# The high and low parts of turned tiles take a place in the weights' line beside w_down's first tiles

## The chip, the cores and the metric

The kernel runs on one core of a Trainium2 chip. A core has five engines with instruction queues of their own: TensorE (PE; its weight loads are shown as PEld), VectorE (DVE), ScalarE (ACT), GpSimd (POOL) and SyncE (SP). PE multiplies into PSUM; DVE and ACT do elementwise work; SP, ACT and POOL issue DMA transfers, and here nearly all loads of weights are issued by SP. The metric is the device time of the whole program in microseconds, the median of several runs.

## What is computed

One decoder layer on 256 tokens of width 2048, in float32. The parts that matter here are the last two lines, cut from the reference:

```python
h = h + rmsnorm(mix, norm_mix_post)                       # mixer: SSD heads beside attention heads
ff = squared_relu_mlp(rmsnorm(h, norm_mlp_pre), w_up, w_down)
h = h + rmsnorm(ff, norm_mlp_post)

def squared_relu_mlp(u, w_up, w_down):
    hdn = relu(u @ w_up)          # 2048 -> 8192
    return (hdn * hdn) @ w_down   # 8192 -> 2048
```

## The kernel before

**Products of parts.** Every float32 product is made of three products of shortened parts. A matrix is split into a high part, rounded by ACT (line 150), and a low part, the rest, which DVE subtracts (line 151): `split`. PE then adds high x high, high x low and low x high. Weights arrive in pairs of 128-row blocks (a k-pair) by 512 columns, 512 KB, in a buffer named `raw` or in one lent from elsewhere (`ha`, `uc`, `mw`). Their parts go into `hi` and `lo`, of which there are five pairs.

**Two kinds of tiles.** A k-pair is multiplied either directly (`row_tiles`: 24 matmuls for two column blocks and two blocks of tokens) or by Strassen's seven products (`seven`: 21 matmuls). A Strassen tile loads a block `raw_a` for one set of columns and `raw_b` for the other; the first piece of raw_b comes from a buffer in DRAM (`pair`) in which POOL has added two blocks ahead of time. DVE makes sums `e` and `t4` of these blocks (line 275), and four splits follow. The sums of the activations are made by `sums_of_acts` (lines 428 to 431).

**Units.** `unit` works through one pair of column blocks: an order of k-pairs, some direct and some by Strassen, then a few last ones directly; before these, the Strassen sums are combined (`combine_new`, `combine_onto`). The layer's MLP runs in two halves of 4096 hidden columns. In each half units for w_up follow one another, then two units for w_down; the second one of the second half ends the kernel. The first w_down unit of each half has 14 k-pairs in its order and the k-pairs 14 and 15 as last ones.

**Turned tiles.** The hidden activations leave w_up with tokens along the partitions; w_down needs them with features there. A unit for w_up leaves four tiles, two blocks of tokens by two of columns. Each is worked on in two steps (`turned`, a generator): `pump_beside` starts it (ReLU and square on ACT, a copy on ACT that puts the 16-bit halves of its words into a buffer named `halves`, and a DMA transposition issued by SP), and `land_beside` finishes it (a copy back into `halves`, then a `split` of the whole tile, 128x512, into the activations' high and low parts, named `sh`/`sl` or `ah`/`al`). This is done beside the tiles of the next unit, at places given by `TURNS` and `LANDS`. The four tiles of the last w_up unit of a half are started and finished beside the first w_down unit, the landings standing behind its tiles 5, 7, 9 and 11. These units have orders longer than seven, and for them `room["exact"]` is true; the landing behind tile 0 has it false, and so have those beside w_up.

**The order of the instructions.** The program is written in one order, and a planner sorts each engine's queue by priority and by when it expects operands. `tc.high_priority(offset=AHEAD)` lifts what stands in it; all work on weights stands in such a block. Beside that there is a line: `split_in_line` and `add_in_line` put an instruction behind the last ACT and the last DVE instruction of the line (`tc.issue_after`), and become the last ones themselves. All weights that `fetch_next` brings are split in the line. With `room["exact"]`, the two copies of a turned tile are in the line as well (line 1515 in `perhaps_in_line`), with high priority; without it, they are not (line 1512). The split of the turned tile is not in the line, nor has it high priority: it only stands behind the newest ACT instruction of the line when it is written.

**Buffers.** `fetch_next` walks a ring of four `raw` buffers and the lent ones in `room["raw"]`. In the second half's first w_down unit `room["chain"]` is set: each transfer is issued behind the one before. When the last of the four turned tiles has landed, `more_in_place` adds the two buffers that held `halves` to this ring (`spare_a`, `of_halves`). The k-pair behind the fourth landing is k = 12, the one after it the Strassen tile k = 13.

Of the kernel before, what the change touches and what calls it, by code (L numbers as in the profile page):

```python
# [10 lines left out]
F32 = mybir.dt.float32  # L11
# [33 lines left out]
AHEAD = 1_000_000  # L45
# [35 lines left out]
def hymba_layer(ctx: ExitStack, tc: tile.TileContext, x, norm_mix_pre, w_in, conv_w, conv_b, dt_bias, a_log,  # L81
# [34 lines left out]
    def part(k):  # L116
        if k < NK:
            return sh, sl, k
        i, r = divmod(k - NK, NK // 2)
        return (*att[i], r)  # L120
# [26 lines left out]
    def split(hi, lo, src, scale=None):  # L147

        if scale is None:
            return (nc.scalar.activation(hi, src, AF.Copy),  # L150
                    nc.vector.tensor_tensor(lo, src, hi.bitcast(F32), op=ALU.subtract))  # L151
        return (nc.scalar.activation(hi, src, AF.Copy, scale=scale),
                nc.vector.scalar_tensor_tensor(lo, src, scale, hi.bitcast(F32), op0=ALU.mult, op1=ALU.subtract))
# [27 lines left out]
    room = {}  # L181
# [78 lines left out]
    @contextmanager  # L260
    def in_line():

        with ExitStack() as order:
            for last in line.values():
                order.enter_context(tc.issue_after(last.ins))
            yield

    def split_in_line(hi, lo, raw):
        with in_line():
            line["act"], line["dve"] = split(hi, lo, raw)  # L270
            newest["act"] = line["act"]
# [683 lines left out]
    def attention(ap, h, qT, kT, v):  # L955
# [30 lines left out]
        for j, p in enumerate(turned):  # L986
            pair[j] = ap.tile([P, 3 * P], F32, name="pT", bufs=4)
            nc.scalar.activation(pair[j], p[:, :3 * P], AF.Copy)
# [181 lines left out]
    def mix_to_up(c0, ks, acc):  # L1170
# [38 lines left out]
        def turn(t, n):  # L1209
            if len(banks) < 3:  # L1210
                banks.append([bank() if banks else psmall() for _ in range(2)])
            p = turned[t, n] = banks[len(turned) % 3]
            for f in range(4):
                k = 4 * n + f
                nc.tensor.transpose(p[f % 2][:, f // 2 * P:(f // 2 + 1) * P], of_h(t, slice(k * P, (k + 1) * P)), ident)
# [284 lines left out]
    def up_end(fb, b):  # L1500

        def at_end(t, acc):
            with tc.high_priority(offset=AHEAD):
                r = room["shared"][b][t]
                nc.vector.tensor_tensor(r, acc, r, op=ALU.subtract if b else ALU.add)
            beside.append(turned(t, 4 * fb, r))
        return at_end

    def perhaps_in_line(dst, src):

        if not room["exact"]:
            nc.scalar.activation(dst, src, AF.Copy)
            return
        with tc.high_priority(offset=AHEAD), in_line():
            newest["act"] = line["act"] = nc.scalar.activation(dst, src, AF.Copy)

    def turned(t, k, r):
        room["halves"].rotate(1)
        halves = room["halves"][0]
        ts = slice(t * P, (t + 1) * P)  # L1520
        words = r.bitcast(U16)
        nc.scalar.activation(r, r, AF.Relu, scale=rmlp[:, t:t + 1])
        nc.scalar.activation(r, r, AF.Square)
        perhaps_in_line(halves.rearrange("p (h n) -> p h n", h=2), words.rearrange("p (n h) -> p h n", h=2))
        nc.sync.dma_start_transpose(words.rearrange("p (n s) -> p n s", s=P), halves)
        yield
        perhaps_in_line(halves.rearrange("p (n h) -> p h n", h=2), words.rearrange("p (h n) -> p h n", h=2))
        d_h, d_l, i = part(k)
        split(d_h[:, i:i + 4, ts], d_l[:, i:i + 4, ts], halves.bitcast(F32).rearrange("p (f s) -> p f s", f=4))

    def onto_new_mw(more):

# [98 lines left out]
```

## Time and profile before

| | us |
|---|---|
| median of 3 runs | 1460.96 (1460.77 to 1460.99) |
| the profiled execution | 1460.29 |
| its span, first to last instruction | 1458.5 |
| PE busy in the span | 1437.7 |
| DVE busy | 1297.9 |
| ACT busy | 1001.3 |
| w_down's first unit of the first half, PE | about 937.5 to 1026.7 |
| the same of the second half | about 1272.5 to 1367.9 |

The profile is of one execution. A row of a timeline gives start and duration in microseconds, the engine, the line of the code, the operation, what is written and read, the shape and a count; the brackets at its end tell how long the engine was idle ahead of it and what ended that. A row of waits gives who waited for whom, the total, the number of times and the longest. A row "<- DMA" names a transfer; SPq is SP's queue of transfers. A line can be that of a helper: 150 and 151 are all splits, and the tiles' names tell which.

### The profile page before, as it was taken

The numbers are of one execution on the slowest core, as the hardware profiler recorded it, in microseconds if no ns is written. First come the engines' busy times: TensorE is split into PE (matmuls) and PEld (weight loads), VectorE is DVE, ScalarE is ACT, GpSimd is POOL, SyncE is SP. The second block draws the span as 40 slices with busy tenths as digits, with TensorE's granted clock in tenths as the row PEclk, the third lists the DMA queues.
The fourth block names the chain that finished last, engine by engine and source line by source line (L and its number), as shares of the span: only waits on it lengthen the run. The fifth ranks groups of instructions, "written<-read, shape, count | busy, mean of one in ns | idle before, by whom it ended". The sixth has DMA issues, their size and how long they took to land.

```text
span 1458.5 us, 20230 instructions
## 1 busy us (share of the span) xinstructions
PE 1437.7 (99%) x6930; PEld 1207.1 (83%) x6930; DVE 1297.9 (89%) x1881; ACT 1001.3 (69%) x1407; POOL 162.3 (11%) x244
## 2 busy tenths in 40 slices
PE   9999999999999999999999999999999999998998
PEld 8888888888888888888888888887888888876786
DVE  6798888988999788689989999999889999987998
ACT  6577669666666666566657679976565799876564
POOL 0201110131111000011100111010111111001000
PEclk9999999999999999999999999999999999999999
DMA  7977656756888647588976799698788999998855
GB/s 256 276 218 225 186 173 185 238 173 195 235 249 244 196 131 237 183 270 262 267 232 211 222 342 291 186 256 273 203 252 263 266 268 278 254 259 250 275 181 173
DMA packets 201926, 340.30 MB, mean 233 GB/s; under 512 B 45616, under 2 KB 48544, under 8 KB 201824
## 3 DMA queue, kind: packets, MB, share of 16 engines
q1 hardware_dynamic: 174304, 279.72, 61.4%
q0 software_dynamic: 19648, 45.63, 15.5%
q10 hardware_dynamic: 7872, 13.68, 2.8%
q8 instruction: 54, 0.88, 0.2%
q14 instruction: 48, 0.39, 0.1%
HBM read 327.39 MB, written 49.84 MB: 259 GB/s over the span
## 4 chain that ended last, share of the span: by engine, by line
PE 65%; DVE 6%; ACT 3%; issue 2%; DMA 2%; SPq 0%; DVEq 0%; ACTq 0%
PE acc L384 9%; PE acc L382 9%; PE acc L383 9%; PE acc L469 6%; PE acc L470 6%; PE acc L471 6%; PE acc L540 4%; DVE lo L151 3%; PE ps L384 2%; PE ps L382 2%; PE ps L383 2%; PE acc L543 2%; PE ps L471 2%; PE ps L470 2%; PE ps L469 2%
## 5 line engine op out<-in xcount | busy, mean ns | idle before, releaser
L151 DVE TENSOR_TENSOR lo<-raw,hi 128x1024 fp32r<-128x1024 f32 (+1 forms) x392 | 475.4, 1217 | 84.6 <-ACT hi L150 82.5
L150 ACT ACTIVATE hi<-raw 128x1024 fp32r<-128x1024 f32 (+1 forms) x392 | 408.0, 1048 | 181.6 <-PE acc L384 58.1
L540 PE MATMUL acc<-ua,hi 128*128 128x512 f32 x520 | 142.1, 402 | 0.0
L150 ACT ACTIVATE hi<-e 128x1024 fp32r<-128x1024 f32 x66 | 70.0, 1061 | 61.0 <-DVE e L275 55.5
L540 PEld LDWEIGHTS acc<-ua,hi 128*128 128x128 f32 x520 | 91.8, 190 | 14.1
L382 PE MATMUL acc<-hi,ua 128*128 128x512 f32 x228 | 90.0, 395 | 0.0
L383 PE MATMUL acc<-lo,ua 128*128 128x512 f32 x228 | 89.2, 391 | 0.0
L384 PE MATMUL acc<-hi,ua 128*128 128x512 f32 x228 | 89.1, 391 | 0.0
L382 PE MATMUL acc<-hi,sh 128*128 128x512 f32 x220 | 86.4, 393 | 0.0
L384 PE MATMUL acc<-hi,sl 128*128 128x512 f32 x220 | 85.7, 389 | 0.0
L383 PE MATMUL acc<-lo,sh 128*128 128x512 f32 x220 | 85.6, 389 | 0.0
L543 PEld LDWEIGHTS acc<-ua,lo 128*128 128x128 f32 x520 | 77.0, 190 | 9.0
L151 DVE TENSOR_TENSOR lo<-e,hi 128x1024 fp32r<-128x1024 f32 x66 | 80.4, 1217 | 0.9 <-ACT hi L150 0.7
L543 PE MATMUL acc<-ua,lo 128*128 128x256 f32 x520 | 79.2, 282 | 0.0
L469 PE MATMUL acc<-hi,ah 128*128 128x512 f32 x180 | 70.1, 390 | 4.1 <-ACT hi L150 4.1
L470 PE MATMUL acc<-lo,ah 128*128 128x512 f32 x180 | 70.4, 391 | 0.0
L471 PE MATMUL acc<-hi,al 128*128 128x512 f32 x180 | 70.3, 390 | 0.0
L540 PE MATMUL acc<-uc,hi 128*128 128x512 f32 x208 | 61.4, 405 | 0.0
L150 ACT ACTIVATE hi<-ha 128x1024 fp32r<-128x1024 f32 x46 | 48.2, 1051 | 15.8 <-DMA ha<-in_w_down_dram 6.2
L151 DVE TENSOR_TENSOR lo<-ha,hi 128x1024 fp32r<-128x1024 f32 x46 | 55.7, 1218 | 2.7 <-ACT hi L150 2.6
L150 ACT ACTIVATE hi<-r 128x512 fp32r<-128x512 f32 x66 | 41.2, 625 | 18.3 <-PE acc L384 8.5
L469 PE MATMUL acc<-hi,ua 128*128 128x512 f32 x137 | 53.5, 390 | 0.0
(578 smaller groups left out, 3739.0 us busy)
## 6 DMA issues: line engine op xcount, KB each, us to landing
raw<-in_w_in_dram SPq DMA_DIRECT2D x154, 512.0 KB, 4.6
raw<-in_w_down_dram SPq DMA_DIRECT2D x70, 512.0 KB, 5.4
raw<-in_w_up_dram SPq DMA_DIRECT2D x65, 512.0 KB, 5.1
raw<-in_w_out_dram SPq DMA_DIRECT2D x38, 512.0 KB, 5.1
raw<-pair SPq DMA_DIRECT2D x61, 256.0 KB, 4.3
pair<-in_w_up_dram POOLq DMA_DIRECT2D x56, 256.0 KB, 6.1
pair<-in_w_down_dram POOLq DMA_DIRECT2D x52, 256.0 KB, 5.8
ha<-in_w_up_dram SPq DMA_DIRECT2D x25, 512.0 KB, 5.7
```

The costliest lines, as they stand in the source:

```text
L150: return (nc.scalar.activation(hi, src, AF.Copy), nc.vector.tensor_tensor(lo, src, hi.bitcast(F32), op=ALU.subtract))
L151: nc.vector.tensor_tensor(lo, src, hi.bitcast(F32), op=ALU.subtract))
L382: nc.tensor.matmul(dst[:, cs], a_h[:, r, ts], hi[:, j, cs], start=begin and j == 0, stop=False)
L383: nc.tensor.matmul(dst[:, cs], a_h[:, r, ts], lo[:, j, cs], start=False, stop=False)
L384: product[t] = nc.tensor.matmul(dst[:, cs], a_l[:, r, ts], hi[:, j, cs], start=False, stop=end and j == KB - 1)
L469: nc.tensor.matmul(dst, a_h, hi[:, j], start=own and first, stop=False)
L470: nc.tensor.matmul(dst, a_h, lo[:, j], start=False, stop=False)
L471: nc.tensor.matmul(dst, a_l, hi[:, j], start=False, stop=own and last)
L540: nc.tensor.matmul(acc[f], hi[:, j, f * P:(f + 1) * P], u(k0 + j), start=k0 + j == 0, stop=False, skip_group_check=True)
L543: nc.tensor.matmul(acc[f][:, 0], lo[:, j, f * P:(f + 1) * P], u(k0 + j)[:, 0], start=False, stop=k0 + j == NK - 1, skip_group_check=True)
```

## The change

When `room["exact"]` is set, the split of a landed turned tile is made by `split_in_line` in a block of high priority; otherwise it is made as before.

```diff
         yield
         perhaps_in_line(halves.rearrange("p (n h) -> p h n", h=2), words.rearrange("p (h n) -> p h n", h=2))
         d_h, d_l, i = part(k)
-        split(d_h[:, i:i + 4, ts], d_l[:, i:i + 4, ts], halves.bitcast(F32).rearrange("p (f s) -> p f s", f=4))
+        whole = halves.bitcast(F32).rearrange("p (f s) -> p f s", f=4)
+        if not room["exact"]:
+            split(d_h[:, i:i + 4, ts], d_l[:, i:i + 4, ts], whole)
+            return
+        with tc.high_priority(offset=AHEAD):
+            split_in_line(d_h[:, i:i + 4, ts], d_l[:, i:i + 4, ts], whole)
```

`split_in_line` is as it was:

```python
def split_in_line(hi, lo, raw):
    with in_line():
        line["act"], line["dve"] = split(hi, lo, raw)
        newest["act"] = line["act"]
```

## The prediction

> **What bounds the kernel now.** The profiled execution took 1460.29 us; its span is 1458.5. I read the page first, then what TensorE (PE) waited for over the whole span, then the timelines around its longest waits on PE, VectorE (DVE), ScalarE (ACT) and SP's DMA queue.
>
> ```profile
> span 1458.5 us, 20230 instructions
> PE 1437.7 (99%) x6930; PEld 1207.1 (83%) x6930; DVE 1297.9 (89%) x1881; ACT 1001.3 (69%) x1407; POOL 162.3 (11%) x244
> ...
> PE acc L469 <- ACT hi L150: 5.7, 2, 4.1
> PE ps L384 <- DVE al L151: 3.4, 1, 3.4
> PE ps L383 <- DVE lo L151: 2.2, 4, 0.8
> ```
>
> PE bounds nearly everything. Two places carry most of its waits: one of 3.4 us for `al`, the low part of a turned tile, and two of 5.7 us together for high parts of weights. The first lies beside the first w_down tiles of the first half, the others beside those of the second half, just where turned tiles are split. First half, PE's timeline, then two stretches (busy times, granted clock, DMA share, GB/s):
>
> ```profile
> 1011.92 0.39 PE L382 MATMUL acc<-hi,ah 128*128 128x512 f32 x1
> 1012.15 0.39 PE L383 MATMUL acc<-lo,ah 128*128 128x512 f32 x1
> 1015.98 0.50 PE L384 MATMUL ps<-hi,al 128*128 128x512 f32 x1 [3.44 <-DVE al L151]
> 1020.66 0.39 PE L384 MATMUL ps<-hi,al 128*128 128x512 f32 x1
> ...
> 1016.00:1020.00 4.00, 4.00 (x12) 3.14 (x13) 2.54 (x5) 1.65 (x2) 0.55 (x1) 0.64 0.95 337
> 1303.00:1307.00 4.00, 2.92 (x12) 1.88 (x11) 3.17 (x7) 4.00 (x5) 0.55 (x1) 1.00 0.91 287
> ```
>
> Unhindered matmuls start about every 0.227 us (the first two rows, rounded there). From 1012.15 to 1020.66 lie 14 starts, worth 3.18 us, in 8.51: **5.3 us are lost**, 3.6 in the gap and 1.7 in a stretch at 0.64 of the clock. The second stretch holds the longest wait on a weight's low part, 0.8 us, and kept the clock at 1.00. What ACT and DVE did:
>
> ```profile
> 989.91 0.61 ACT L150 ACTIVATE ah<-mw 128x512 fp32r<-128x512 f32 x1
> 999.76 0.61 ACT L150 ACTIVATE ah<-mw 128x512 fp32r<-128x512 f32 x1
> ...
> 1010.15 2.35 DVE L151 TENSOR_TENSOR lo<-raw,hi 128x1024 fp32r<-128x1024 f32 x2
> 1014.10 1.22 DVE L151 TENSOR_TENSOR lo<-raw,hi 128x1024 fp32r<-128x1024 f32 x1 [1.60 <-ACT hi L150]
> 1015.24 1.28 DVE L151 TENSOR_TENSOR al<-mw,ah 128x512 fp32r<-128x512 f32 x2
> ```
>
> Both high parts were ready by 1000.4, yet their low parts stand behind every low part of weights, even one (1014.10) that waited for its own high part and belongs to the next unit: this unit's last four are the ones up to 1012.5. PE waited for 1.28 us of work that could have been done over 10 us earlier. Second half:
>
> ```profile
> 1343.39 0.39 PE L384 MATMUL acc<-hi,al 128*128 128x512 f32 x1
> 1347.89 0.50 PE L469 MATMUL acc<-hi,ah 128*128 128x512 f32 x1 [4.11 <-ACT hi L150]
> 1350.36 0.80 PE L469 MATMUL acc<-hi,ub 128*128 128x512 f32 x1 [1.55 <-ACT hi L150]
> 1355.16 0.39 PE L470 MATMUL acc<-lo,ub 128*128 128x512 f32 x1
> ...
> 1352.00:1355.00 3.00, 3.00 (x9) 2.32 (x8) 1.77 (x3) 2.49 (x3) 0.80 (x1) 0.50 0.94 327
> ...
> 1333.51 1.37 ACT L1515 ACTIVATE ha<-wpost 128x1024 uint16<-128x1024 uint16 x1
> 1336.62 0.61 ACT L150 ACTIVATE ah<-ha 128x512 fp32r<-128x512 f32 x1
> 1346.78 1.06 ACT L150 ACTIVATE hi<-ha 128x1024 fp32r<-128x1024 f32 x1 [6.17 <-DMA ha<-in_w_down_dram]
> ...
> 1335.04 0.68 DVE L151 TENSOR_TENSOR lo<-r,hi 128x512 fp32r<-128x512 f32 x1
> 1339.06 0.68 DVE L151 TENSOR_TENSOR al<-ha,ah 128x512 fp32r<-128x512 f32 x1
> 1339.86 0.68 DVE L151 TENSOR_TENSOR al<-ha,ah 128x512 fp32r<-128x512 f32 x1
> 1350.82 1.22 DVE L151 TENSOR_TENSOR lo<-e,hi 128x1024 fp32r<-128x1024 f32 x1
> ...
> 1338.96 0.37 SPq L164 DMA_DIRECT2D ha<-in_w_down_dram  x1
> 1340.57 0.37 SPq L164 DMA_DIRECT2D ha<-in_w_down_dram  x1
> SPq L164 <- DVE al L151: 1.2, 1, 1.2
> 1341.49 6.88 DMA raw<-in_w_down_dram
> ```
>
> Here the lateness acts through SP. After the fourth landing the buffers through which tiles were turned become weight buffers, and the next Strassen tile's raw_a (k = 13) goes into one of them. Its transfer was issued at 1340.57, right behind the last `al`; raw_b is chained behind it, and its second piece, issued at 1341.49, took 6.88 us. From 1343.39 to 1355.16 lie 14 starts, worth 3.18 us, in 11.77: **8.6 us are lost**, waits and half the clock together. SP had issued the transfer at 1338.96, one for the next unit, ahead of it.
>
> **The change part by part.** Eight pairs of splits, four in each half, get high priority and a place in the line: the high part on ACT right behind the copy back (L1515, in the line already), the low part on DVE in the weights' order. No instruction and no DMA is added or removed.
>
> The first two pairs of each half follow their copies closely already. They change places with neighbours whose sum stays the same: nothing. The third and fourth move.
>
> *The first half's wait.* Both `al` would be done near 1000. What is late next are the low parts of this unit's last weights, done at 1012.5, or 1.2 later with the push below; PE then has most of 40 matmuls (9 us) ahead of the last of them, which covers it. Gain 5.3.
>
> *The push.* Two low parts move ahead of weights on a DVE that runs there without a gap; each costs 0.60 (1.28 less the 0.68 of one). The rows of the k-pair behind the fourth landing:
>
> ```profile
> 998.45 1.22 DVE L151 TENSOR_TENSOR lo<-mw,hi 128x1024 fp32r<-128x1024 f32 x1
> 1000.36 0.39 PE L382 MATMUL ps<-hi,ah 128*128 128x512 f32 x1
> ...
> 1336.25 1.22 DVE L151 TENSOR_TENSOR lo<-ha,hi 128x1024 fp32r<-128x1024 f32 x1
> 1338.18 0.39 PE L382 MATMUL ps<-hi,ah 128*128 128x512 f32 x1
> ```
>
> With 1.2 more the low part ends at 1000.87, and PE's second matmul wants it at 1000.59: a wait of 0.3. In the second half 1338.67 against 1338.41, again 0.3. Bounds of each: 0, if low-priority sums give way, and 1.2, all of the push. ACT's high parts move too, by some 0.5 each, hidden in the 31% that ACT is idle; without that cover it is the same push once more.
>
> *The transfer.* The fourth copy ends at 1334.9. Behind it come its high part and, after the low part that now ends near 1336.3, its `al`, done near 1336.9 in place of 1340.54. raw_a goes out at 1337.0, raw_b's second piece at 1337.9, as far behind as before. The planner can issue raw_a as soon as its model sees the buffer free, and the line frees it ahead of the k = 12 weights' buffers, for which the next unit's transfers wait. How long the piece then takes:
>
> ```profile
> raw<-in_w_down_dram SPq DMA_DIRECT2D x19, 256.0 KB, 4.7
> ```
>
> Between 4.7 (median of its kind) and 6.88; I take 5.5, since fewer transfers stand ahead of it. It lands at 1343.4. Before, the low part of `e` ended 3.67 after that landing (1350.82 + 1.22 less 1348.37): 1347.1. At full speed PE wants it at 1343.39 + 0.23 + 0.3 + 7 x 0.227 = 1345.5. A wait of 1.6 stays, 0.8 to 3.0 by the bounds. Whether a wait of 1.6 costs clock no row shows; 0.8 did not and 3.4 did, for 1.7. It is nearer to 0.8, so 0, with 1.7 as the other end.
>
> The Trainium skill (TensorE: Matmul & The Clock Gate, "HAM oscillation — how this bites in real kernels") warns of PE gaps above about 3.4 us and not of shorter ones. By that the remaining wait has no such tail and the sum stands; a gate that acts at 1.6 already would make it 10.0. The trace agrees at both ends, 0.8 and 3.4.
>
> *The sum.* 5.3 + 8.6 - 0.3 - 0.3 - 1.6 = **11.7 us**. Span 1446.8, that execution 1448.6, and the median of the runs, 0.67 above it, **1449.3**. With all costs at their lower ends the gain is 13.1 (1447.9); at their upper ends, 5.3 + 8.6 - 1.2 - 1.2 - 3.0 - 1.7 = 6.8 (1454.2).
>
> That the first half's 5.3 reaches the end needs the weights to keep ahead of an earlier PE. ACT's waits from 1040 to 1060 and from 1360 to 1380:
>
> ```profile
> ACT hi L150 <- PE acc L384: 4.9, 4, 2.1
> ACT hi L150 <- PE acc L384: 4.5, 3, 1.7
> ```
>
> Behind both places ACT waits for PE to free weight buffers. Preparation is as far ahead as its buffers allow, so everything later moves with PE.
>
> **The rivals.** *SP keeps its order* (0.13): the planner leaves raw_a behind the transfer at 1338.96, whose buffer is pushed by 1.2; raw_a gains nothing, the second half loses 8.6 as before. Gain 5.3 - 0.6 = 4.7: 1456.3. For it speaks that the planner did put that transfer first; against it, that the buffer is now free earlier in any model, since the line fixes it.
>
> *The first gain is swallowed* (0.09) by the up phase of the second half, where DVE is nearly full: gain 11.7 - 5.0 = 6.7, 1454.3. Against it stand the waits for buffers.
>
> *It does not do what it says* (0.07): the low parts stay where they are, because the planner still sees their copies late. 1461. Against it: L1515 is the in-line copy, and the splits take their order from it.
>
> *Slower* (0.06): the line holds both engines at a late copy. Now DVE's weights, too, queue behind an `al` that waits for a copy that waits for its transposition. Each of eight landings would cost PE the lateness; above 1.5 us each (11.7 / 8) the kernel is slower. SP's transpositions of the second half already waited for ACT, 2.2 us each:
>
> ```profile
> SPq L1525 <- ACT hi L150: 8.9, 4, 3.8
> ```
>
> At 2.2 each, 1449.3 + 17.6 = 1466.9. Against it: the copy at 1333.51 has no idle time before it. The Trainium skill (TensorE: Matmul & The Clock Gate, opening table) calls the queues of ACT and DVE strict FIFO, which is what would make this bite; the first half's `al` behind a waiting low part agrees.
>
> **How the numbers follow.** The forecast has 0.65, with a range of its own from 1446 to 1454. The range from 1445 to 1457.5 adds the first two rivals and, below, the chance that the small waits for low parts (2.2 us) shrink too; it leaves out the last two and a little more. Faster, same and slower mean by more than 0.2%, 2.9 us, about what can be told here: 0.86, 0.08, 0.06.
>
> **What would show it.** Right: no PE wait for `al`; each `al` within 2 us behind its high part; raw_a's issue before 1338 and before the next unit's second transfer; no stretch under full clock near 1016 or 1350; small new waits for low parts behind the landings. Wrong: a DMA wait over 3 us at k = 13 (SP's order), new waits of PE in the up phase of the second half (swallowed), or idle ACT time before L1515 (the slower rival).

## The result, and the profile after

The changed kernel takes **1449.95 us** (median of 4 runs, 1449.0 to 1453.54) against 1460.97 (4 runs, 1460.77 to 1462.45): a ratio of 0.9927, 95% interval 0.9908 to 0.9946. That is 11.0 us faster. The profiled execution took 1449.0. Timed again on another chip, the same kernel had 1450.74 (6 runs) against 1459.61 (18 runs), 0.9946 (0.9931 to 0.9962), so 8.9 us. The gain is sure; its size is known to some 3 us either way.

The page of the changed kernel, span and busy times:

```profile
span 1446.7 us, 20233 instructions
...
PE 1432.2 (99%) x6930; PEld 1202.3 (83%) x6930; DVE 1298.3 (90%) x1881; ACT 1002.8 (69%) x1407; POOL 162.4 (11%) x244
```

What PE waited for (in total, times, longest):

```profile
PE acc L469 <- ACT hi L150: 2.3, 2, 1.5
PE ps L382 <- ACT hi L150: 1.9, 3, 0.7
PE ps L383 <- DVE lo L151: 1.8, 3, 0.8
```

The same work is done. DVE, ACT and POOL are busy as long as before, to within 1.5 us. PE is busy for 5.5 us less (1437.7 before): from the first w_down unit on, the old profile had two stretches at half clock, 3.41 and 6.83 us long, and this one has none. The row for `al` is gone, the waits of L469 have shrunk from 5.7 to 2.3, and those of L382 have grown (0.7 before).

**Where the 11.8 us between the two spans lie.** The first matmul of three units is easy to find in both timelines: w_down's first unit of the first half, the unit that follows it, and w_down's first unit of the second half. Before:

```profile
937.50 0.39 PE L382 MATMUL ps<-hi,sh 128*128 128x512 f32 x1
...
1026.80 0.39 PE L382 MATMUL acc<-hi,sh 128*128 128x512 f32 x1
...
1272.47 0.39 PE L382 MATMUL ps<-hi,sh 128*128 128x512 f32 x1
```

After:

```profile
936.05 0.39 PE L382 MATMUL ps<-hi,sh 128*128 128x512 f32 x1
...
1020.91 0.39 PE L382 MATMUL acc<-hi,sh 128*128 128x512 f32 x1
...
1266.62 0.39 PE L382 MATMUL ps<-hi,sh 128*128 128x512 f32 x1
```

The differences of these starts, and what is left up to the span's end:

| us | before | after | gain |
|---|---|---|---|
| start to the first place | 937.50 | 936.05 | 1.45 |
| first place (w_down's first unit) | 89.30 | 84.86 | 4.44 |
| between (second unit, up phase) | 245.67 | 245.71 | -0.04 |
| second place to the end | 186.03 | 180.08 | 5.95 |

The first 1.45 us lie ahead of all changed instructions: the old kernel's profiled execution had a slower start. The other profiles start this place between 935.03 and 936.09, whether their kernel has the change or not. So the 1.45 us aren't the change's, and the two places gave 10.4 us between these two executions.

**The first place.** The changed kernel's timeline on ACT, DVE and PE at the fourth landing, and two stretches of PE's time where the old kernel waited until 1015.98 and then ran at 0.64 of the clock (busy times, granted clock, DMA share, GB/s):

```profile
997.06 0.63 ACT L150 ACTIVATE ah<-mw 128x512 fp32r<-128x512 f32 x1
998.41 0.68 DVE L151 TENSOR_TENSOR al<-mw,ah 128x512 fp32r<-128x512 f32 x1
999.35 1.22 DVE L151 TENSOR_TENSOR lo<-mw,hi 128x1024 fp32r<-128x1024 f32 x1
999.62 0.62 PE L382 MATMUL ps<-hi,ah 128*128 128x512 f32 x2
1000.07 0.61 PE L382 MATMUL acc<-hi,ah 128*128 128x512 f32 x2
1000.60 0.50 PE L469 MATMUL acc<-hi,ah 128*128 128x512 f32 x1
1000.93 0.39 PE L383 MATMUL ps<-lo,ah 128*128 128x512 f32 x1
```

```profile
1008.00:1012.00 4.00, 4.00 (x19) 3.34 (x18) 4.00 (x7) 2.92 (x3) 0.00 (x0) 1.00 0.99 252
1012.00:1016.00 4.00, 4.00 (x20) 3.30 (x19) 4.00 (x5) 1.67 (x2) 0.00 (x0) 1.00 0.52 165
```

`al` is done at 999.1, not at 1016.5, and PE is busy without a gap at full clock. The weights' low part now ends at 1000.57, and no wait stands before the matmul that wants it at 1000.93: five products of high parts come first, where the old order had one.

**The second place.** The chain of waits of the changed kernel (start, duration, what):

```profile
1330.45 0.70 DVE al L151
...
1331.16 0.37 SPq L164
...
1331.59 0.46 SPq L159
...
1332.09 6.80 DMA raw<-in_w_down_dram
...
1338.99 0.70 DVE e L275
...
1339.78 1.07 ACT hi L150
...
1340.89 0.50 PE acc L469
```

The same stretch on PE's timeline, and the granted clock behind it:

```profile
1337.48 0.39 PE L384 MATMUL acc<-hi,al 128*128 128x512 f32 x1
1338.63 0.50 PE L469 MATMUL acc<-hi,ah 128*128 128x512 f32 x1 [0.77 <-ACT hi L150]
...
1340.89 0.50 PE L469 MATMUL acc<-hi,ub 128*128 128x512 f32 x1 [1.52 <-ACT hi L150]
...
1343.50 0.39 PE L470 MATMUL acc<-lo,ub 128*128 128x512 f32 x1
```

```profile
1339.00:1342.00 3.00, 1.48 (x7) 0.94 (x6) 3.00 (x4) 2.22 (x3) 0.00 (x0) 1.00 1.05 405
1342.00:1345.00 3.00, 3.00 (x15) 2.46 (x14) 3.00 (x5) 3.00 (x5) 0.29 (x1) 1.00 1.05 412
```

raw_a goes out right behind `al`, but the chain is the old one: `al`, raw_a, raw_b's second piece, `e`, PE. From 1337.48 to 1343.50 lie the 14 starts that took 11.77 us; now they take 6.02, and less 3.18 (their worth unhindered) that is a loss of 2.8 us in place of 8.6, all at full clock.

### The profile page after: what moved, and what is told of

Read it like the earlier page. It is cut to its first block, busy times and chain, and to the rows that moved or that the text cites. A ratio compares the mean times of both kernels' runs of the same rounds, so it can differ in the third digit from the quotient of the medians.

```text
span 1446.7 us, 20233 instructions
## 1 busy us (share of the span) xinstructions
PE 1432.2 (99%) x6930; PEld 1202.3 (83%) x6930; DVE 1298.3 (90%) x1881; ACT 1002.8 (69%) x1407; POOL 162.4 (11%) x244
## 4 chain that ended last, share of the span: by engine, by line
PE 61%; DVE 6%; ACT 5%; issue 3%; DMA 2%; SPq 0%; ACTq 0%; DVEq 0%
PE acc L382 8%; PE acc L383 8%; PE acc L384 8%; PE acc L469 5%; PE acc L470 5%; PE acc L471 5%; PE acc L540 4%; DVE lo L151 3%; ACT hi L150 3%; PE ps L383 2%; PE ps L384 2%; PE ps L382 2%; PE ps L470 2%; PE ps L471 2%; PE ps L469 2%
## 5 line engine op out<-in xcount | busy, mean ns | idle before, releaser
L540 PEld LDWEIGHTS acc<-ua,hi 128*128 128x128 f32 x520 | 91.3, 189 | 14.3 <-ACT hi L150 0.3
L382 PE MATMUL acc<-hi,ua 128*128 128x512 f32 x228 | 90.1, 395 | 0.0
L384 PE MATMUL acc<-hi,ua 128*128 128x512 f32 x228 | 89.0, 391 | 0.0
L382 PE MATMUL acc<-hi,sh 128*128 128x512 f32 x220 | 86.4, 393 | 0.0
L469 PE MATMUL acc<-hi,ah 128*128 128x512 f32 x180 | 70.2, 390 | 0.8 <-ACT hi L150 0.8
L469 PE MATMUL acc<-hi,ua 128*128 128x512 f32 x137 | 53.5, 390 | 0.0
L471 PE MATMUL acc<-hi,ua 128*128 128x512 f32 x137 | 53.3, 389 | 0.0
```

The lines of the kernel that those rows point to most:

```text
L382: nc.tensor.matmul(dst[:, cs], a_h[:, r, ts], hi[:, j, cs], start=begin and j == 0, stop=False)
L384: product[t] = nc.tensor.matmul(dst[:, cs], a_l[:, r, ts], hi[:, j, cs], start=False, stop=end and j == KB - 1)
L469: nc.tensor.matmul(dst, a_h, hi[:, j], start=own and first, stop=False)
L471: nc.tensor.matmul(dst, a_l, hi[:, j], start=False, stop=own and last)
L540: nc.tensor.matmul(acc[f], hi[:, j, f * P:(f + 1) * P], u(k0 + j), start=k0 + j == 0, stop=False, skip_group_check=True)
```

## The experiments

The theory is the prediction's: the third and fourth `al` are late; in the first half PE waits for one of them, in the second half the transfer of raw_a into the buffer that held `halves` does. Each experiment's ratio is to the kernel before on the same chip.

### Each half alone

```diff
-        if not room["exact"]:
+        if not (room["exact"] and room["half"] == 0):
```

`room["half"]` is set to the half's number; the other run has `== 1`.

> Only the first half's four landed tiles are split in the line; the second half is as before. Theory (two separate losses, 5.3 and 8.6 us, both from late low parts, and everything behind the first half moves with PE): no PE wait for al near 1016, the waits at k = 13 of the second half stay (4.1 and 1.5 us), gain 4.7 to 5.3, 1456 us. Rival (the first half's gain is swallowed in the up phase, all of the gain is the second half's): 1460 to 1461.

> Only the second half's four landed tiles are split in the line. Theory: the wait of 3.4 us for al near 1016 stays with its slow stretch, the second half's waits shrink to about 2 us, gain 6 to 7, 1454 us; with the kernel that does only the first half it adds up to the whole change's 11 us. Rival (first half's gain swallowed): 1449 to 1450 by this half alone.

The first half alone: 1454.22 (5 runs) against 1460.09, ratio 0.9964 (0.9951 to 0.9977), a gain of 5.9 us. The second half alone: 1455.46 (10 runs), 0.9973 (0.9963 to 0.9982), a gain of 4.6. Together 10.5, about the whole. Each lies outside what was expected of it (4.7 to 5.3, and 6 to 7), the one above and the other below. PE's timeline with the first half alone:

```profile
1341.51 0.79 PE L469 MATMUL acc<-hi,ah 128*128 128x512 f32 x1 [4.52 <-ACT hi L150]
```

and with the second half alone:

```profile
1014.49 0.80 PE L384 MATMUL ps<-hi,al 128*128 128x512 f32 x1 [4.38 <-DVE al L151]
```

Each place keeps its old wait where it is left alone, so they are independent. By the same differences of starts the first place takes 84.88 us where its half is changed and 90.86 where not; from the second place to the end it is 184.88 where not changed and 182.10 where changed. The gain of the first half isn't swallowed: the stretch between is 245.72 and 245.69. The second half gave less than the prediction's 6.7. In its profile the clock was at half there twice, for 3.41 us each time: behind two waits at the first landing, and behind the two that stay at k = 13 (1.17 and 1.39 us). As PE was busy throughout both, that is some 3.4 us lost. The prediction had put this term at nothing at k = 13 and had none at the first landing. The first of the two, with the clock behind it:

```profile
1303.81 0.50 PE L382 MATMUL ps<-hi,sh 128*128 128x512 f32 x1 [0.77 <-ACT hi L150]
1305.07 0.50 PE L383 MATMUL ps<-lo,sh 128*128 128x512 f32 x1 [0.76 <-DVE lo L151]
```

```profile
1306.00:1309.00 3.00, 3.00 (x9) 2.31 (x8) 2.96 (x4) 1.00 (x2) 0.00 (x0) 0.50 1.58 338
```

### The buffer at k = 13

Behind the second half's fourth landing only `spare_a` is lent to the weights, not the buffer that held `halves`. Once this is done to the old kernel, once to the changed one.

```diff
-        room["raw"] += [spare_a, room["of_halves"]]
+        room["raw"] += [spare_a]
```

> The kernel before with one edit: the buffer of the last two turned tiles is not lent to weights, so raw_a of k = 13 goes to a raw buffer that is free long before; the splits stay late. Theory (the second half's loss comes from that buffer alone): the wait of 4.1 us and the slow stretch at k = 13 vanish, the first half's 3.4 us stay, gain 7 to 8.6, 1452.5 to 1454; the last unit has other buffers, which may cost or give some tenths. Rival (the transfer is late for another reason, its rate or SP's queue): 1460 to 1461.

> The changed kernel once more, for its spread and as the base of the runs beside it: 1449 to 1451.

> The changed kernel, and the buffer of the last two turned tiles is not lent to weights, so raw_a of k = 13 has a buffer that is free early. With late splits this edit alone gave nothing (the low parts went to the very end of the queue of DVE instead). Theory (with the splits early, the 2.3 us that PE still waits at k = 13 come from that transfer): these waits go, 2 us faster than the changed kernel, 1448. Rival (DVE is full there and sets the pace; the wait only moves behind k = 13): no difference from the changed kernel.

In the old kernel it changed **nothing**: 1459.71 (10 runs), ratio 1.0001 (0.9991 to 1.001). In the changed kernel it gave **1445.84** (5 runs, 1445.53 to 1447.12), ratio 0.9912 (0.9897 to 0.9927), against 0.9946 for the changed kernel beside it: 4.9 us less. SP's queue in the changed kernel with this edit, and the largest of what its PE waited for:

```profile
1317.04 0.37 SPq L164 DMA_DIRECT2D raw<-in_w_down_dram  x1
1319.27 0.34 SPq L159 DMA_DIRECT2D raw<-pair  x1
1319.66 0.42 SPq L160 DMA_DIRECT2D raw<-in_w_down_dram  x1
```

```profile
PE ps L382 <- ACT hi L150: 2.8, 3, 1.6
```

raw_b goes out at 1319.3 and 1319.7, over 12 us earlier than in the changed kernel (1331.6, 1332.1), and the wait of L469 is gone. From the second place to the end it is 178.25, against 180.08 and 182.49 in the two profiles of the changed kernel. Against the first of them, the 2.8 lost at k = 13 are gone and a longer wait at the first landing (1.57 in place of 0.65) takes some of it back. The 4.9 of the times is more than that and more than the 2 expected. How it divides is open; the granted clock of the runs points to less time at half clock (1.0 in three of these five, 0.996 to 0.999 in the changed kernel's six). The old kernel with the same edit had these transfers early too (1325.9), and no wait at k = 13. What it had instead, on ACT (the last copy), DVE and PE:

```profile
1334.32 1.36 ACT L1515 ACTIVATE ha<-wpost 128x1024 uint16<-128x1024 uint16 x1
...
1356.97 1.28 DVE L151 TENSOR_TENSOR al<-ha,ah 128x512 fp32r<-128x512 f32 x2
```

```profile
1353.03 0.73 PE L383 MATMUL acc<-lo,ah 128*128 128x512 f32 x2 [1.53 <-DVE lo L151]
1356.50 0.79 PE L383 MATMUL acc<-lo,sh 128*128 128x512 f32 x1 [2.74 <-DVE lo L151]
...
1359.22 0.62 PE L384 MATMUL ps<-hi,al 128*128 128x512 f32 x1
```

Once the transfer no longer needs them, the two `al` stand behind every low part of this unit's weights, over 20 us behind the last copy. The products with `al` were moved to the end, and PE ran out of other work and waited for the last weights' low parts: the first half's trouble, in another form, came up in the second. With the low parts early, the same edit shows no such wait. So the transfer was only the way in which the late `al` acted first; the root is its place in DVE's order. The buffer pays only once that is mended.

### Priority alone, line alone

The change does two things to the split, and these do one each:

```diff
         with tc.high_priority(offset=AHEAD):
-            split_in_line(d_h[:, i:i + 4, ts], d_l[:, i:i + 4, ts], whole)
+            split(d_h[:, i:i + 4, ts], d_l[:, i:i + 4, ts], whole)
```

```diff
-        with tc.high_priority(offset=AHEAD):
+        if True:
             split_in_line(d_h[:, i:i + 4, ts], d_l[:, i:i + 4, ts], whole)
```

> The changed kernel without the place in the line: the split of a landed tile has high priority only. Theory (the lateness of al came from its low priority, and either measure alone cures it): no PE wait for al, two waits for high parts at k = 13 of about 2 us together, and a time of 1449 to 1451, within 1.5 us of the changed kernel. Rival (the place in the line is what does it, priority alone leaves al behind weights whose operands the planner sees earlier): a wait for al of over 2 us comes back, 1455 to 1460.

> The changed kernel without the high priority: the split of a landed tile has its place in the line only. Theory (either measure alone cures it): the weights behind it in the line can't be planned before it, so it is planned early, 1449 to 1451, no PE wait for al. Rival (only the priority does it): without it the whole line waits until the planner takes a low-priority instruction, so that weights come late as well: waits for high and low parts of weights behind each landing of over 1 us, 1455 to 1467.

Priority alone: 1452.02 (4 runs) against 1459.47, ratio 0.9949 (0.9931 to 0.9966). Line alone: 1451.2 (4 runs), 0.9943 (0.9928 to 0.9959). Both lie a little above the 1449 to 1451 that was expected. Neither can be told from the changed kernel's 0.9946, and neither has a wait for `al`; the first place takes 85.05 and 84.85 us. Either measure cures the order by itself. Priority alone had, in its profile, one wait at k = 13 in place of two, and the clock fell there:

```profile
1340.81 0.80 PE L469 MATMUL acc<-hi,ub 128*128 128x512 f32 x1 [2.85 <-ACT hi L150]
```

```profile
1337.00:1340.00 3.00, 0.88 (x3) 0.30 (x2) 1.53 (x3) 0.48 (x2) 0.50 (x1) 0.93 1.03 373
1340.00:1344.00 4.00, 3.19 (x8) 2.54 (x9) 4.00 (x5) 3.73 (x6) 0.80 (x1) 0.50 1.05 410
1344.00:1348.00 4.00, 4.00 (x14) 3.21 (x13) 1.46 (x3) 2.20 (x4) 0.00 (x0) 0.70 1.08 352
```

### The last two landings alone, and with the other buffer

```diff
-        if not room["exact"]:
+        if not (room["exact"] and k == 28):
```

> Only the third and fourth landed tile of each half are split in the line; the first two are split as before. Theory (the first two change places with neighbours of the same sum, only the last two matter): the changed kernel's time, 1449 to 1451. Rival (all eight matter): a gain of about half, 1455. A third reading, that putting the first two in the line costs some tenths by delaying ReLU and square and so the next copy: up to 1 us faster than the changed kernel.

> The changed kernel with two edits together: only the third and fourth landing of each half are split in the line, and behind the second half's fourth landing only the buffer spare_a is lent to the weights, not the one that held halves. Nothing is left out of the computation. Theory (the two edits act at different places, and the first two landings give nothing either way): no wait at k = 13, and the time of the changed kernel with the other buffer, 1445 to 1447. Rival (the first two landings in the line cost something at late copies, as the 3.1 us wait of one profile at the second half's first landing suggests): 1 to 3 us less than that, 1442 to 1445.

Alone: 1449.58 (4 runs) against 1460.09, ratio 0.9933 (0.9914 to 0.9952), the changed kernel's within the error. So the first two landings bring nothing, and all of the gain is the last two. With the other buffer: **1445.2** (4 runs, 1444.88 to 1446.01), 0.9901 (0.9887 to 0.9916), the lowest median of all these kernels and 14.3 us below the old one beside it, though its interval doesn't part it from 0.9912 with all four landings in the line. The rival of one to three microseconds more isn't settled by it.

### Later turns

To make copies late on purpose, the turns of the four tiles were started behind later tiles, once in the old and once in the changed kernel.

```diff
-TURNS = ((1, 2, 4, 5), (3, 4, 6, 8))
+TURNS = ((1, 2, 4, 5), (4, 6, 8, 10))
```

> The kernel before with tiles started one or two places later in the long orders (behind tiles 4, 6, 8, 10 in place of 3, 4, 6, 8), landings unmoved, so that the copies back come about 9 us behind the transpositions' start in place of 19. Both theories: ACT's copies now wait for transpositions, and as the copies are in the line already here, weights wait with them: slower by some us, 1462 to 1468.

> The same with the changed kernel. The slower rival (a late copy now holds DVE too, for the low part stands in its line): slower than the changed kernel by clearly more than the other pair differs, so that the change's gain of 11 us shrinks to under 6. Theory (DVE's next weight needs ACT's next high part, which stands behind the copy anyway, so the line on DVE adds nothing): both lose about the same, the gain stays 9 to 12.

1463.02 (8 runs) and 1453.63 (7 runs), ratios 1.0021 (1.0004 to 1.0037) and 0.9963 (0.9951 to 0.9975): both some 3 us slower, the change still worth 9.4. In the profiles most of this lies in the first place, which takes 92.21 and 87.33 us, against 89.30 and 84.86. But the edit failed at its aim: ACT waited for a transposition for 0.6 us altogether in the one and not at all in the other. It gives no price for a late copy. The repeat of the changed kernel did, by chance; its ACT and PE at the second half's first landing, and the clock behind it:

```profile
1295.33 1.37 ACT L1515 ACTIVATE ha<-hb 128x1024 uint16<-128x1024 uint16 x1 [2.82 <-DMA hb<-ha]
```

```profile
1300.72 0.80 PE L382 MATMUL ps<-hi,sh 128*128 128x512 f32 x1 [3.07 <-ACT hi L150]
```

```profile
1303.00:1306.00 3.00, 3.00 (x9) 2.32 (x8) 2.96 (x4) 1.00 (x2) 0.81 (x1) 0.50 1.25 259
```

A copy 2.8 us late cost 3.1 us of PE and then half the clock. The same landing was late by 1.0 in the first profile of the changed kernel and by 1.4 with only the last two landings in the line (and the other buffer), where that landing's split isn't in the line; the old kernel with the other buffer had 1.4 there too. The copy itself is in the line in every one of these kernels. So it can be late without the line of the splits, and without PE's arrival some 6 us earlier. Of the eleven profiles with the turns unchanged, only the old kernel's has this copy in time. What makes it late is open.

## Why the prediction came out

The time was 1449.3 on paper and 1449.95 and 1450.74 in the two measurements, and the mechanisms were the ones named. But the sum's 11.7 is near the spans' 11.8 partly by luck: 10.4 came from the two places and 1.45 from a start that the change doesn't touch. There is luck in the times too: with one half changed at a time, the first gave 5.9 where 5.0 was on paper and the second 4.6 where it was 6.7, two misses that partly cancel. Step by step:

- **The first half's wait (5.3): right.** The wait and its half clock are gone. The first place as a whole gave 4.44, and 5.9 by the run that changed that half alone, with 5.0 (5.3 less the push) predicted.
- **"The first two pairs ... nothing": wrong by about half a microsecond in the first half.** There is a new wait for a high part of a weight, 0.56 at the second landing; with only the last two landings in the line it is 0.29. In the times it doesn't show.
- **The push (0.3 in each half): didn't come.** In the first half the low part of the weight ended at 1000.57, later by 1.6 against PE's own shift of 0.74 than before (999.67), so the push was above the 1.2 assumed. It cost nothing, because more products of high parts stood ahead: the lower bound, "if low-priority sums give way", for another reason. In the second half no wait stands there either.
- **The transfer (7.0 net): the right chain, one term mis-sized.** Set PE's start 1337.48 against 1343.39, a shift of 5.91, and add it to the new times: `al` is done at 1337.1 (predicted 1336.9), raw_b's second piece goes out at 1338.0 (1337.9), and the low part of `e` ends 3.67 us behind its landing, as predicted. The mis-sized term is the transfer: **6.80 us, not 5.5**, no faster than the 6.88 of before. That made the remaining loss 2.8 in place of 1.6; the two waits are for the high parts of raw_a and of `e`, where a wait for the low part of `e` was expected. In this profile the upper bound, 6.88, was the right value. It isn't fixed: with only the last two landings in the line the same piece took 5.33 us, and one wait of 1.70 stood there. So the reason given for 5.5, fewer transfers ahead of it, did not hold in this profile.
- **Clock behind the remaining wait (0): right in both profiles of the changed kernel, not in general.** There the two waits, 2.3 and 1.9 us together, cost no clock. At the same place, two of 1.17 and 1.39 with the second half alone did, for 3.41 us, or 1.7 lost. One of 2.85 in the run with priority alone did too, and from 1340.8 on the clock was at half until about 1346.4 (2.4 us of the 4 up to 1348 by the 0.70), some 2.8 us lost; the bound of 1.7 was too low. The Trainium skill (TensorE: Matmul & The Clock Gate, "HAM oscillation — how this bites in real kernels") puts the harm at gaps above about 3.4 us; these runs show it behind two waits of 0.77 and 0.76 us (second half alone, first landing), and there the measurement decides. That it stayed away from the changed kernel's k = 13 is partly luck.
- **The first gain passes through: right, exactly.** 245.67 and 245.71 between the places.

The rivals. That SP keeps its order fell: raw_a's issue at 1331.16 stands ahead of the next unit's second transfer at 1337.51. The swallowed gain fell by the stretch between the places. That the change does nothing fell with the wait for `al`. The slower one, a late copy that holds both engines, has a true core, with 3.1 us at one landing in one profile; but in both profiles of the changed kernel only one landing of eight was late, and the 1.5 us at each that it needed never came.

The prediction was right that the late `al` acts through the buffer. What the expectation for the other buffer in the old kernel had wrong is that the buffer can be priced by itself: that run removed the transfer's wait and gained nothing, because `al` then came later still.

## What to carry to other kernels

A product's low part that is cheap and ready early, but ranked behind work that keeps its engine full, is done last; one place in the order, by priority or by a chain, was enough to mend it here. When a late result holds a buffer, take both away before pricing either: here, freeing the buffer alone only let the planner put the result still later. Check a gain between two profiles at landmarks ahead of the edit, since executions differ there by a microsecond or two (935.03 to 937.50 in these).

## What was not expected of the hardware

The clock fell after shorter waits than thought. Waits of PE that lie within about 3 us of each other, and the granted clock behind them:

| kernel | waits, us | clock behind |
|---|---|---|
| changed, k = 13 | 0.77 + 1.52 | 1.00 |
| changed, other buffer, first landing | 1.57 + 0.76 | 1.00 |
| old kernel, other buffer, first landing | 1.79 + 0.76 | 1.00 |
| second half alone, first landing | 0.77 + 0.76 | 0.50 |
| second half alone, k = 13 | 1.17 + 1.39 | 0.50 |
| line alone, first landing | 2.02 + 0.76 | 0.50 |
| priority alone, k = 13 | 2.85 | 0.50 |
| old kernel, first half | 3.44 | 0.64 in 4 us |

The row of the line alone, the waits and the stretch behind:

```profile
1299.91 0.49 PE L382 MATMUL ps<-hi,sh 128*128 128x512 f32 x1 [2.02 <-ACT hi L150]
1301.17 0.79 PE L383 MATMUL ps<-lo,sh 128*128 128x512 f32 x1 [0.76 <-DVE lo L151]
```

```profile
1300.00:1303.00 3.00, 2.24 (x5) 1.58 (x6) 3.00 (x4) 2.27 (x3) 0.00 (x0) 0.59 1.01 363
1303.00:1306.00 3.00, 3.00 (x8) 2.31 (x7) 2.96 (x5) 1.73 (x2) 0.64 (x1) 0.50 1.33 255
```

When the clock falls isn't a fixed time behind the start of a wait. With the line alone, 0.59 as the mean of full and half puts the fall at 1300.5, after the wait of 2.02 was over and in the further 0.76. With priority alone, 0.93 between 1337 and 1340 puts it at 1339.6, only 1.6 us into the wait. So a limit on the length of one gap doesn't describe what these runs show, and neither does one on the sum of two waits: 1.53 in two lost the clock and 2.55 in two kept it.

What the traces do show is a grid. In eight of the profiles there are 13 stretches at half clock from 960 us on, and each lasted 3.41, 6.83 or 10.24 us, to 0.01. Within one profile they begin whole multiples of 3.413 us apart: at 1017.16 and 1348.25 in the old kernel (97 times), at 1306.01 and 1346.97 with the second half alone (12 times). If time from 960 to 1400 is cut at these marks, PE was idle for 1.52 us or more in the piece just ahead of every fall, and for at most 1.45 us in every other piece at full clock. So the same waits cost nothing or a whole stretch, by where they lie between two marks. This is read off these profiles; no run varied it by itself, and the five profiles without a fall don't show where their marks are.
